# Last product of an encoder layer: quadrant sums of the first visits written into the output tiles, residual added in the second visits

## The chip, the core and the metric

The kernel runs on one core of a Trainium2 chip. The metric is device time in microseconds (us) of one execution; lower is better. Line numbers (L1215 is line 1215) are those of the kernel before the change.

## What is computed

One layer of an encoder over two sequences of 512 tokens with 1024 features: a state-space branch, a differential attention and a cross attention, merged by gates, then a feed-forward part. The change touches the last product of the feed-forward part alone:

```python
x = x + merged @ p['w_out'][l]                       # the residual: x1 in the kernel
xn2 = _rmsnorm(x, p['norm_ffn'][l])
gate, up = jnp.split(xn2 @ p['w_ffn_in'][l], 2, axis=-1)
return x + (jax.nn.silu(gate) * up) @ p['w_ffn_out'][l]   # d_ff = 2816; then a final rmsnorm
```

All arithmetic is in float32. A product is made of three matmuls on split operands (high part times high, high times low, low times high).

## The kernel before

**Data.** Activations lie transposed: 128 features on the partitions, and 1024 columns (two sequences of 512) in a tile. The sum x + merged @ w_out is made tile by tile and kept in device memory as `x1D[0..7]`. The hidden activations of the feed-forward part lie in device memory as `aD[0..21]`.

**The last product** multiplies 22 tiles of hidden activations by `w_ffn_out` into eight output tiles `y[0..7]` (128x1024 each, in four double tiles of the tag `yo`). Eighteen of the 22 hidden tiles go in nine pairs through a scheme of Strassen-Winograd kind: with a pair p of hidden tiles and a pair (m, m+4) of output tiles, seven 512-column products give the four quadrants, a quadrant being one output tile in one sequence. A step with one (m, p) is a **piece**: seven products of three matmuls, so 21 matmuls of 128x128 by 128x512. The last four hidden tiles are multiplied afterwards in the ordinary way (L1240 to L1305), together with the final norm.

**Visits.** `VISITS` (L35) lists twelve visits (m, first pair, end of pairs); below they are called v0 to v11. v0 to v3 are the first visits of m = 0..3 (pairs from 0 on, 2 to 4 pieces), v4 to v7 the second ones (3 pieces each), v8 to v11 the third ones. There are 36 pieces. In a visit seven PSUM banks (six of the tag `mm`, one of `tr`) collect the seven products over the pieces of the visit. Then they are drained (`quadrants`, L1068): ScalarE copies the first bank to `p1`, and seven VectorE additions (`summed`, L1062 to L1066, one PSUM operand and one SBUF operand each) leave the four quadrant sums c11, c22, c21 and c12 in scratch tiles: one of `gf`, one of `up`, two of `nsq`, each tag with two buffers. GpSimd then adds each of the four into its half of `y[m]` or `y[m+4]` (L1213 to L1215, four additions of 128x512 a visit). TensorE starts the next visit while the drain goes on; it needs a bank only when its own turn comes.

**Residual.** In each first visit at pair 1 (L1200 to L1203) two DMAs of 512 KB put `x1D[m]` and `x1D[m+4]` into `y[m]` and `y[m+4]`, so that all quadrant sums are added onto the residual.

**Pairs.** `act_pair` (L1081) loads two hidden tiles (`fa`, `fb`) into the tag `ld`, a ring of four 128x1024 tiles, and makes four sums of quadrants in the tile `ts` (`quad_sums`, L931 to L939: three VectorE operations at L935, L937 and L938, one GpSimd operation at L936). `quad_split` (L947) splits all seven operands into high (ScalarE, L132) and low parts (VectorE, L133). Nine pairs pass in this way; seven of them during the visits. In the text, pair 3's `fb` is the second tile of the fourth pair. After v8 the ring holds the last four hidden tiles (`fl`, L1231).

**Weights.** Pieces 0 to 15 load seven ready-made weight matrices from `wD` (two DMAs, L1165 and L1167). Pieces 16 to 27 load four of the seven, and the raw weights for the other three (L418, L422), which are split on the core (L135 on ScalarE, L136 on VectorE). Pieces 28 to 35 load raw weights alone, whose sums GpSimd makes (L427 to L430). Six tiles (`w_room`, L1150) hold the weights of three pieces, so the load for piece n can go out when piece n-3 is done.

**Order.** All DMAs of this stage are issued by the queue of SyncE (SP), strictly one after the other: a DMA that waits for its tile holds back all that stand behind it. The order in each engine's queue is worked out at build time by a scheduler with a simulated timeline, so an instruction may stand well ahead of its place in the text; `tc.issue_after(i)` keeps an instruction behind i on i's engine, and `queued()` (L283) keeps a DMA behind the last weight load. TensorE's order in the visits is fixed by the text (`PE.on`).

## Time and profile before

| | us |
|---|---|
| median of three runs (lowest, highest) | 1623.96 (1622.52, 1624.75) |
| the profiled execution's own time | 1623.77 |
| its span, first to last instruction | 1622.0 |
| TensorE busy | 1588.7 (98%) |
| VectorE busy | 1170.7 (72%) |
| GpSimd busy | 548.8 (34%) |

The granted TensorE clock of the profiled execution was 0.995 of full speed. Times in the trace count from the start of the span; about 1.8 us of the execution's own time lie outside it. The visits lie between about 1385 and 1564 us. Busy time counts how long instructions ran; TensorE's matmuls are pipelined, so a matmul of 0.39 us may start 0.23 us after the one before. "<-" in a row names what an operation reads, or, behind an idle time, what ended it.

### The profile page before, as it was taken

Reading aid. Unit: us, or ns where it says so; the run is one execution under the profiler, and the core shown is the slowest. Engines: PE = TensorE matmul, PEld = TensorE weight load, DVE = VectorE, ACT = ScalarE, POOL = GpSimd, SP = SyncE. Lnnn points to the kernel's source line nnn. Section 1 sums busy time; section 2 is a strip of 40 time slices with the busy share of each in tenths; the row PEclk is TensorE's granted clock in tenths of the full one; section 3 lists DMA queues with packets and bytes.
Section 4 is the critical chain, followed back from the end, with each engine's and each line's share of the span. In section 5 each row is a group of like instructions: output and inputs, shape, how many; then the busy total and the mean of one; then the engine's idle time right before and its main releaser. Section 6 shows DMA issues by size and latency. Waiting matters only on the chain.

```text
span 1622.0 us, 21561 instructions
## 1 busy us (share of the span) xinstructions
PE 1588.7 (98%) x7812; PEld 1312.7 (81%) x7812; DVE 1170.7 (72%) x1852; ACT 639.0 (39%) x1141; POOL 548.8 (34%) x452
## 2 busy tenths in 40 slices
PE   7999999999999999999999999999999999999997
PEld 6788788888898778777878888888888887777877
DVE  8957897067774666767364668888898877988664
ACT  6534323265553355564123444333233233233233
POOL 0001100000223221300343367666655554444563
PEclk9999999999999999999999999999999999999998
DMA  9354533666763110144454532333333223885322
GB/s 378 119 170 157 147 130 120 180 221 229 247 210 129 53 59 27 50 146 168 139 187 136 154 101 97 126 121 117 119 115 117 83 87 114 324 338 184 98 66 104
DMA packets 104747, 237.84 MB, mean 147 GB/s; under 512 B 13505, under 2 KB 44993, under 8 KB 104641
## 3 DMA queue, kind: packets, MB, share of 16 engines
q1 hardware_dynamic: 104640, 236.47, 42.7%
q8 instruction: 61, 1.00, 0.3%
q14 instruction: 46, 0.37, 0.1%
HBM read 165.16 MB, written 71.27 MB: 146 GB/s over the span
## 4 chain that ended last, share of the span: by engine, by line
PE 74%; DVE 12%; DMA 5%; issue 4%; POOL 2%; ACT 2%; SPq 0%; DVEq 0%; POOLq 0%; ACTq 0%
PE bkmm L64 64%; PE bksc L64 2%; PE bkoo L64 2%; PE bktr L67 2%; DVE wl L133 1%; DVE st L1580 1%; PE bktr L64 1%; DMA yt<-bD 1%; PE bktr L1562 1%; DMA w<-wD 1%; POOL mg L760 1%; DVE tl L133 1%; POOL y L1215 1%; DMA fa<-aD 0%; DMA wf<-in_w_mv 0%
## 5 line engine op out<-in xcount | busy, mean ns | idle before, releaser
L64 PE MATMUL bkmm<-xh,wh 128*128 128x512 f32 x640 | 255.6, 399 | 1.2 <-ACT wh L132 1.2
L64 PE MATMUL bkmm<-xh,wl 128*128 128x512 f32 x640 | 250.8, 392 | 0.0
L64 PE MATMUL bkmm<-xl,wh 128*128 128x512 f32 x640 | 250.7, 392 | 0.0
L64 PE MATMUL bkmm<-th,wl 128*128 128x512 f32 (+1 forms) x621 | 241.3, 389 | 3.0 <-DVE wl L133 3.0
L64 PE MATMUL bkmm<-tl,wh 128*128 128x512 f32 (+1 forms) x621 | 241.8, 389 | 0.6 <-DVE tl L133 0.6
L64 PE MATMUL bkmm<-th,wh 128*128 128x512 f32 (+1 forms) x621 | 241.6, 389 | 0.7 <-ACT th L132 0.7
L132 ACT CAST wh<-wf 128x1024 fp32r<-128x1024 f32 (+1 forms) x133 | 117.7, 885 | 200.5 <-PE bkmm L64 174.0
L133 DVE TENSOR_TENSOR wl<-wf,wh 128x1024 fp32r<-128x1024 f32 (+1 forms) x133 | 147.7, 1111 | 63.6 <-ACT wh L132 54.7
L64 PEld LDWEIGHTS bkmm<-xh,wh 128*128 128x128 f32 x640 | 120.3, 188 | 31.9 <-issue 7.9
L64 PE MATMUL bkmm<-th,w 128*128 128x512 f32 x432 | 141.7, 392 | 4.2 <-DMA w<-wD 2.2
L64 PEld LDWEIGHTS bkmm<-xh,wl 128*128 128x128 f32 x640 | 120.2, 188 | 27.0 <-issue 1.3
L64 PEld LDWEIGHTS bkmm<-th,wl 128*128 128x128 f32 x621 | 116.8, 188 | 27.6 <-DVE wl L133 3.5
L64 PEld LDWEIGHTS bkmm<-xl,wh 128*128 128x128 f32 x640 | 120.5, 188 | 22.3 <-issue 0.4
L64 PEld LDWEIGHTS bkmm<-tl,wh 128*128 128x128 f32 x621 | 116.8, 188 | 25.2 <-DVE tl L133 1.3
L64 PEld LDWEIGHTS bkmm<-th,wh 128*128 128x128 f32 x621 | 116.8, 188 | 24.6 <-ACT th L132 0.8
L427 POOL TENSOR_TENSOR raw<-raw 128x128 f32<-128x128 f32 x28 | 14.9, 531 | 294.7 <-DVE hl L136 262.9
L1127 POOL TENSOR_TENSOR up<-up,acc 128x512 f32<-128x512 f32 x44 | 84.2, 1932 | 77.3 <-DVE up L1065 77.3
L64 PEld LDWEIGHTS bkmm<-th,w 128*128 128x128 f32 x432 | 81.0, 188 | 25.5 <-DVE up L1065 3.3
L1126 ACT ACTIVATE ac<-gf 128x512 f32<-128x512 f32 x44 | 27.8, 633 | 163.8 <-DVE gf L1125 82.7
L760 POOL TENSOR_TENSOR mg<-mg,gl 128x1024 f32<-128x1024 f32 x16 | 43.9, 2743 | 140.0 <-DVE gl L756 140.0
L521 ACT ACTIVATE e<-bksc,nb 128x512 f32<-128x512 f32 (+1 forms) x96 | 58.7, 615 | 71.9 <-DVE nb L516 51.7
L64 PE MATMUL bkmm<-tl,w 128*128 128x512 f32 x216 | 84.2, 390 | 0.0
(638 smaller groups left out, 3606.4 us busy)
## 6 DMA issues: line engine op xcount, KB each, us to landing
wf<-in_w_in SPq DMA_DIRECT2D x40, 512.0 KB, 3.8
wD<-hl SPq DMA_DIRECT2D x28, 512.0 KB, 2.9
w<-wD SPq DMA_DIRECT2D x28, 512.0 KB, 4.7
gD<-gt SPq DMA_DIRECT2D x24, 512.0 KB, 2.9
gl<-gD SPq DMA_DIRECT2D x24, 512.0 KB, 3.4
wf<-in_w_fg SPq DMA_DIRECT2D x22, 512.0 KB, 3.5
wf<-in_w_fu SPq DMA_DIRECT2D x22, 512.0 KB, 3.5
aD<-ac SPq DMA_DIRECT2D x22, 512.0 KB, 2.8
```

The costliest lines, as they stand in the source:

```text
L64: return self.put(self.eng.matmul(*args, **kw))
L67: return self.put(self.eng.transpose(*args, **kw))
L132: h = S.copy(hi, src)
L133: l_ = V.tensor_tensor(out=lo, in0=src, in1=hi.bitcast(F32), op=ALU.subtract)
L427: PO.tensor_tensor(out=a22, in0=a21, in1=a22, op=ALU.add)
L521: last_x = S.activation(out=e, in_=sc, func=AF.Exp, bias=nb, scale=scale, accum_out=sm)
L760: PO.tensor_tensor(out=mg[m], in0=mg[m], in1=gt, op=ALU.add)
L1126: last_t = S.activation(out=ac[:, cs], in_=gf, func=AF.Tanh, scale=0.5)
L1127: PO.tensor_tensor(out=up, in0=up, in1=accs[s], op=ALU.mult)
L1215: PO.tensor_tensor(out=yv, in0=yv, in1=c_, op=ALU.add)
L1562: PE.matmul(ps[:, g * P : (g + 1) * P], w_[:, gg * P : (gg + 1) * P], u_[:, 8 * o + gg, :], start=True, stop=True)
L1580: V.tensor_tensor(out=sv[:, :, :, i], in0=p_, in1=q_, op=ALU.add)
```

## The change

In v0 to v3 the four sums that `quadrants` makes are written by VectorE into the halves of `y[m]` and `y[m+4]` themselves; GpSimd adds nothing there, and `x1D` is not loaded. In v4 to v7, from the visit's first piece on, `x1D[m]` and `x1D[m+4]` are loaded into two tiles of the ring `ld`; after the four quadrant additions of these visits GpSimd adds the two tiles onto `y[m]` and `y[m+4]`, each in one addition of 128x1024. v8 to v11 are as before. The other callers of `quadrants` get the same tiles in the same order.

```diff
     def summed(tag, p_, other, bufs=1):
         nonlocal last_sum
-        t_ = (rp if tag == "nsq" else ap2).tile([P, L], F32, tag=tag, name=tag, bufs=bufs)
+        t_ = tag
+        if isinstance(tag, str):
+            t_ = (rp if tag == "nsq" else ap2).tile([P, L], F32, tag=tag, name=tag, bufs=bufs)
         last_sum = V.tensor_tensor(out=t_, in0=p_, in1=other, op=ALU.add)
         return t_
 
-    def quadrants(ps, p0, other=("up", "gf")):
+    def quadrants(ps, p0, names=("gf", "gf", "up", "up")):
...
-        c11 = summed("gf", next(ps), p1, 2)
+        c11 = summed(names[0], next(ps), p1, 2)
...
-        c22 = summed("up", p5, u3, 2)
-        c21 = summed(other[0], next(ps), u3, 2)
-        return c11, summed(other[1], next(ps), u4, 2), c21, c22
+        c22 = summed(names[3], p5, u3, 2)
+        c21 = summed(names[2], next(ps), u3, 2)
+        return c11, summed(names[1], next(ps), u4, 2), c21, c22
...
-            if v < 4 and p == 1:
+            if 4 <= v < 8 and p == lo_:
+
+                xs = [slot("ld", name="xr") for _ in range(2)]
                 with queued():
-                    for t in (m, m + 4):
-                        nc.sync.dma_start(y[t], x1D[t])
+                    for t, x_ in zip((m, m + 4), xs):
+                        nc.sync.dma_start(x_, x1D[t])
...
-        c11, c12, c21, c22 = quadrants(ps, next(ps), ("nsq", "nsq"))
-        for c_, t, s in ((c11, 0, 0), (c22, 4, 1), (c21, 4, 0), (c12, 0, 1)):
-            yv = y[m + t][:, s * L : (s + 1) * L]
-            PO.tensor_tensor(out=yv, in0=yv, in1=c_, op=ALU.add)
+        yv = [y[m + t][:, s * L : (s + 1) * L] for t in (0, 4) for s in range(NS)]
+        if v < 4:
+            quadrants(ps, next(ps), yv)
+        else:
+            c11, c12, c21, c22 = quadrants(ps, next(ps), ("gf", "nsq", "nsq", "up"))
+            for c_, y_ in ((c11, yv[0]), (c22, yv[3]), (c21, yv[2]), (c12, yv[1])):
+                PO.tensor_tensor(out=y_, in0=y_, in1=c_, op=ALU.add)
+            if v < 8:
+                for t, x_ in zip((m, m + 4), xs):
+                    PO.tensor_tensor(out=y[t], in0=y[t], in1=x_, op=ALU.add)
```

## Prediction

> **What bounds the kernel now.** I read the page first, then the busy times of the last product in thirds, then TensorE's instructions in order of time, looking for every start that comes later than the pace.

> ```profile
> span 1622.0 us, 21561 instructions
> PE 1588.7 (98%) x7812; PEld 1312.7 (81%) x7812; DVE 1170.7 (72%) x1852; ACT 639.0 (39%) x1141; POOL 548.8 (34%) x452
> ```

> TensorE (PE) is busy for 98% of the span. The change lies in the visits, from about 1385 to 1564 us. The next view has, for three stretches of them, the busy time of PE, PEld, VectorE (DVE), ScalarE (ACT) and GpSimd (POOL), the granted clock, the share of the DMA engines and GB/s.

> ```profile
> 1385.00:1444.00 59.00, 56.68 (x247) 45.74 (x246) 53.83 (x59) 17.70 (x22) 28.59 (x18) 1.00 0.95 368
> 1444.00:1503.00 59.00, 58.20 (x255) 47.21 (x254) 50.28 (x63) 18.02 (x26) 27.23 (x20) 1.00 0.64 219
> 1503.00:1565.00 62.00, 60.92 (x265) 49.09 (x264) 41.26 (x54) 17.36 (x28) 38.30 (x50) 1.00 0.23 69
> ```

> PE leaves 2.3, 0.8 and 1.1 us open: 4.2 us in 180. So GpSimd's work, which the change moves about, can give no more than PE's own gaps give. In v0 to v3 (first row) two other things are full: the DMA engines (0.95) and VectorE (53.8 of 59). In v4 to v7 the DMA engines have room (0.64). Now the gaps, in TensorE's rows:

> ```profile
> 1390.75 0.39 PE L64 MATMUL bkmm<-th,w 128*128 128x512 f32 x1
> 1392.25 0.50 PE L64 MATMUL bkmm<-th,w 128*128 128x512 f32 x1 [1.11 <-DMA w<-wD]
> ...
> 1425.49 0.39 PE L64 MATMUL bkmm<-tl,w 128*128 128x512 f32 x1
> 1425.72 0.39 PE L64 MATMUL bkmm<-th,w 128*128 128x512 f32 x1
> 1427.23 0.47 PE L64 MATMUL bkmm<-th,w 128*128 128x512 f32 x1 [1.12 <-DMA w<-wD]
> ...
> 1462.71 0.39 PE L64 MATMUL bkmm<-th,w 128*128 128x512 f32 x1
> 1463.85 0.50 PE L64 MATMUL bkmm<-th,w 128*128 128x512 f32 x1 [0.76 <-DVE up L1065]
> ...
> 1506.99 0.39 PE L64 MATMUL bkmm<-th,w 128*128 128x512 f32 x1
> 1507.71 0.50 PE L64 MATMUL bkmm<-th,w 128*128 128x512 f32 x1 [0.32 <-DVE up L1065]
> ```

> The pace is 1425.72 - 1425.49 = 0.23 us from start to start, so a piece of 21 matmuls takes 4.8 us and a visit of three 14.3. Against it the four places lose 1.27 (v0), 1.28 (first piece of v3), 0.91 (first piece of v5) and 0.49 us (first piece of v8): 3.95 us. The first two wait for weights, the other two for VectorE, which has not yet emptied a PSUM bank of the visit before.

> **What is removed: 16 GpSimd additions and eight DMAs in v0 to v3.**

> ```profile
> L1215 POOL TENSOR_TENSOR y<-y,nsq 128x512 f32<-128x512 f32 x22 | 34.8, 1594 | 2.4 <-DVE nsq L1065 2.4
> L1215 POOL TENSOR_TENSOR y<-y,up 128x512 f32<-128x512 f32 x12 | 16.9, 1408 | 10.9 <-DVE up L1065 10.9
> ...
> y<-x1D SPq DMA_DIRECT2D x8, 512.0 KB, 7.0
> ```

> At about 1.5 us each, 16 additions are 24 us of GpSimd. It isn't on TensorE's path there, so by itself that is worth nothing. What counts is whom they hold up. VectorE's rows with a GpSimd addition beside them and without one, and the additions themselves:

> ```profile
> 1399.44 2.31 DVE L133 TENSOR_TENSOR tl<-fb,th 128x1024 fp32r<-128x1024 f32 x1
> 1414.29 2.31 DVE L133 TENSOR_TENSOR tl<-fb,th 128x1024 fp32r<-128x1024 f32 x1
> 1416.52 1.77 DVE L937 TENSOR_TENSOR ts<-fb,ts 128x512 f32<-128x512 f32 x1
> 1418.33 0.69 DVE L938 TENSOR_TENSOR ts<-fb,ts 128x512 f32<-128x512 f32 x1
> 1439.89 1.21 DVE L133 TENSOR_TENSOR tl<-fb,th 128x1024 fp32r<-128x1024 f32 x1
> ...
> 1402.86 2.26 POOL L1215 TENSOR_TENSOR y<-y,nsq 128x512 f32<-128x512 f32 x1
> 1430.44 1.29 POOL L1215 TENSOR_TENSOR y<-y,up 128x512 f32<-128x512 f32 x1
> ```

> The same split takes 1.21 us alone and 2.31 us beside an addition; the addition takes 1.29 alone and 2.26 beside a split. Each loses about what the other needs. Now SP's queue ahead of the second gap:

> ```profile
> 1414.44 0.32 SPq L1084 DMA_DIRECT2D fa<-aD  x1
> 1419.12 0.32 SPq L1085 DMA_DIRECT2D fb<-aD  x1
> 1419.54 0.37 SPq L1167 DMA_DIRECT2D w<-wD  x1
> 1419.96 0.42 SPq L1203 DMA_DIRECT2D y<-x1D  x1
> 1420.48 0.38 SPq L1165 DMA_DIRECT2D w<-wD  x1
> ...
> SPq L1085 <- DVE ts L938: 5.2, 2, 4.3
> ```

> SP stood for 4.3 us at pair 5's `fb`, until L938 of pair 3 had freed its tile. Two weight loads stood behind it, and the second also behind a residual load (512 KB at 368 GB/s: 1.4 us). Those weights came at 1427.1. Without the additions L133 (1414.29) and L937 (1416.52) are 1.1 us shorter each, and so is one L133 of pair 2 ahead of them. I take 3 us less of standing, and 1.4 us less of transfer in front. Gap two needs 1.28. **Gap two goes: -1.3 us** (bounds -1.4 and 0).

> Gap one stays: the first residual load is issued at 1391.42, when the late weights (issued at 1384.78) are almost there. 0 us (bounds -1.3, if the new queue order helps them, and 0).

> VectorE's writes into `y` instead of the scratch tiles have the same size and operands, so 0 us, hidden under TensorE in any case. No one waits for them before v4's additions.

> **What is added: eight loads and eight GpSimd additions of 128x1024 in v4 to v7.** The nearest row of that shape:

> ```profile
> L760 POOL TENSOR_TENSOR mg<-mg,gl 128x1024 f32<-128x1024 f32 x16 | 43.9, 2743 | 140.0 <-DVE gl L756 140.0
> ```

> That is 2 x 2.74 = 5.5 us a visit (bounds 5.2, four times 1.29, and 9.1, four times 2.26). GpSimd has 27.2 us of work in the 59 us of v4 to v7, and gets to 49: it isn't the bound. The loads add 4.2 MB to 59 us at 219 GB/s, which makes 290, under the 368 seen in v0 to v3; 0 us. If they came in front of a late weight load, each would cost it 1.4 us.

> Three things are queued behind the new waits.

> (a) *VectorE beside the longer additions.* Its splits of weights and pairs can each lose up to 2.7 us instead of 1.3. VectorE has 59 - 50.3 = 8.7 us open there, and only the bank drains touch TensorE; an L1065 reads one operand from PSUM and keeps its 0.68 us. I take +0.3 us (bounds 0 and +3).

> [...]

> (b) *The ring `ld`.* The loads take two of its four tiles in each of v4 to v7, so pair 7 has to wait for v5's residual additions and pair 8 for pair 7. In the trace these pairs have long been loaded.

> ```profile
> 1465.12 3.19 POOL L1215 TENSOR_TENSOR y<-y,nsq 128x512 f32<-128x512 f32 x2
> ```

> v4's four additions end at 1468.3. Two residual additions end at 1474 and v5's at 1488. Pair 7 is then loaded by 1494, taking 5 to 6 us, and split by about 1501; pair 8 by 1507 and 1514. Pair 8 is first needed in the fourth piece of v8, which starts after 1507.7 + 2 x 4.8 = 1517 or a little later. Three us are left, so 0 us (bounds 0 and +4).

> (c) *The sums of the pairs in the drains.* The gap of 0.91 us stands where the sums of a pair were put between the drain's additions:

> ```profile
> 1457.10 1.78 DVE L935 TENSOR_TENSOR ts<-fa 128x512 f32<-128x512 f32 x1
> 1458.81 0.68 DVE L1065 TENSOR_TENSOR u<-bkmm,p 128x512 f32<-128x512 f32 x1
> 1461.20 1.39 DVE L938 TENSOR_TENSOR ts<-fb,ts 128x512 f32<-128x512 f32 x1
> 1463.12 0.67 DVE L1065 TENSOR_TENSOR up<-bkmm,u 128x512 f32<-128x512 f32 x1
> ```

> These are pair 7's; they now come two visits later. Gap three goes (-0.9). Gap four, at the start of v8, comes with the work for `fl`, which now also moves back (-0.5). The same sums now lie in the drains of v6 and v7; I take between the two gaps, 0.45 us, for each, +0.9. Net **-0.5 us** (bounds -1.4 and +0.9).

> **Sum.** -1.3 + 0.3 - 0.5 = **-1.5 us**: 1622.3 against the profiled execution's 1623.77, whose span of 1622.0 has 1.8 us around it. The median of the runs is 0.2 us higher, so I give **1622.5 us**; the likeliest case alone reaches from 1621.0 to 1623.3. A measurement of this kernel can tell about 0.2%, 3.2 us, from no change, so this counts as the same.

> **Rivals.**

> *SP stands at a residual load (slower).* In v5 and v7 the new loads wait for GpSimd's residual additions of the visit before. v5 starts at 1460.2 (11 matmuls of 0.23 us before the row of 1462.71); the second of v4's tiles is free at 1474, 13.6 us later. If the queue has the loads where the text has them, behind the third weight load of the visit, all later weights stand there. A weight load may go out two pieces, 9.5 us, ahead of its use, and takes 5.1 us to land:

> ```profile
> w<-wD SPq DMA_DIRECT2D x26, 512.0 KB, 5.1
> ```

> So 4.4 us of standing are free, and the rest, up to 9 us in each of v5 and v7, is TensorE's. It decides from 4.4 us of standing on. Against it: the queue has pair loads where their tiles come free, not where the text has them, and the longest standing at one was 4.3 us. For it: that one cost gap two. With half of the standing in one visit it is 1622.5 + 4.5 = 1627, with all of it in one 1631.5. Chance 0.18.

> *VectorE blocked by the long additions (slightly slower).* Two more blocks of 2.7 us in a visit put 5.4 us on VectorE in each of v4 to v7, 21.6 in all against 8.7 us open. It would be 13 us short if each addition hit a split; a quarter of that, with drains late, is +3: 1625.5. It decides from 8.7 us of blocking on. Chance 0.12. [...]

> *All four gaps go (faster).* The queues are worked out anew, the first weights come ahead of pair 3's loads, and no pair's sums fall into a drain: -3.95, so 1620.0, and with the smaller losses at other drains 1619.3. Chance 0.22.

> *No effect.* Gap two comes from SP's standing alone and stays, or comes back elsewhere: 1623.3 to 1624.5. Chance 0.12.

> **How the numbers follow.** The forecast keeps 0.36. Faster by over 0.2% (under 1620.7) are the third rival and 0.02 of the forecast: 0.24. Slower by over 0.2% (over 1627.2) are most of the first rival, 0.17, and 0.03 of the second: 0.20. The same: 0.56. The range of 1619.3 to 1628.5 leaves out about half of the first rival and a third of the third, near 0.2.

> **What would show it.** In the changed kernel's trace: no TensorE idle put down to DMA w<-wD in v3; DMA share clearly under 0.95 in v0 to v3 and over 0.64 in v4 to v7; L133 near 1.2 us in v0 to v3; residual additions of 2.6 to 3 us; SP's longest standing at a residual load under 4.4 us; pair 8 split before v8's fourth piece. The forecast is wrong if TensorE waits for weights in v5 to v8, for pair 8 in v8, or longer than 1 us for a drain in v4 to v7.

## The result and the profile after

The changed kernel takes 1639.31 us (median; 1637.38 to 1642.51), the kernel before beside it 1622.39 us (1621.32 to 1624.75; six runs of each, three of the six before are those of the table above). The ratio is 1.0103, interval 1.0092 to 1.0114: 17 us slower, outside the range of 1619.3 to 1628.5. The profiled execution took 1637.38 us.

The page of the changed kernel:

```profile
span 1635.6 us, 21557 instructions
PE 1593.0 (97%) x7812; PEld 1313.6 (80%) x7812; DVE 1172.0 (72%) x1852; ACT 639.1 (39%) x1141; POOL 552.9 (34%) x444
```

The busy times hardly moved; the span grew by 13.6 us. Up to the visits both kernels issue the same instructions in the same order, and yet this execution is 5 us ahead of the one before when the visits begin (1380.0 against 1385.2). The other kernels of this document share that part too, and in their traces the visits begin at 1381 to 1385 us, so I take the 5 us as scatter. Traces are therefore compared below by the **length of the visits**, from TensorE's first matmul of the first piece to its first matmul behind the last piece: 178.8 us before, 197.5 us after, +18.7.

Where they lie is seen by cutting both traces at the start of v4. The view gives the busy times of a stretch (length; PE, PEld, DVE, ACT, POOL; clock, DMA share, GB/s). v4 to v11 of the kernel before:

```profile
1445.60:1564.00 118.40, 116.52 (x507) 94.13 (x506) 89.10 (x112) 34.87 (x53) 63.62 (x67) 1.00 0.42 140
```

and of the changed kernel:

```profile
1439.30:1577.40 138.10, 124.49 (x506) 97.28 (x505) 97.63 (x111) 34.27 (x53) 85.91 (x72) 0.95 0.48 161
```

v4 to v11 became 19.7 us longer, v0 to v3 1.1 us shorter (60.4 to 59.3). Of the 19.7 us, 11.7 are time in which PE stands (138.10 - 124.49 = 13.6, against 1.9), and 8.0 are more busy time of the same matmuls. The clock of 0.95 in place of 1.00 accounts, by my estimate, for at most 6.9 of these 8.0 (0.05 of 138.1). GpSimd has 22.3 us more work, VectorE 8.5.

v0 to v3 and v4 to v7 of the changed kernel, for the DMA shares:

```profile
1380.00:1439.00 59.00, 57.71 (x252) 46.62 (x251) 50.19 (x64) 17.70 (x22) 9.56 (x6) 1.00 0.79 281
1439.00:1505.00 66.00, 59.33 (x244) 47.46 (x243) 44.50 (x50) 14.43 (x22) 37.84 (x20) 0.95 0.64 222
```

The DMA share fell from 0.95 to 0.79 in v0 to v3, as forecast. In v4 to v7 it stayed at 0.64, where more was forecast. DMA bandwidth is not what ran out. The waits, from 1380 to 1580 us (total, times, longest), of the changed kernel:

```profile
ACT th L132 <- DMA fa<-aD: 19.1, 4, 12.0
DVE ts L935 <- DMA fa<-aD: 11.2, 3, 7.0
ACT th L135 <- DMA fl<-aD: 9.0, 2, 7.2
PE bkmm L64 <- DVE u L1067: 4.4, 3, 2.2
PE bkmm L64 <- ACT p L1073: 4.0, 1, 4.0
...
PE bkmm L64 <- DVE up L1067: 3.1, 2, 2.9
PE bkmm L64 <- DMA w<-wD: 1.1, 1, 1.1
```

and of the kernel before (1380 to 1565 us):

```profile
ACT th L132 <- DMA fa<-aD: 2.6, 1, 2.6
PE bkmm L64 <- DMA w<-wD: 2.2, 2, 1.1
PE bkmm L64 <- DVE up L1065: 1.2, 3, 0.8
```

One of the two weight waits is gone: gap two. In its place ScalarE and VectorE wait for pairs (`fa`) and for the last tiles (`fl`), and TensorE waits for the drain (L1067 and L1073 are L1065 and L1071 of before; lines behind them have moved as well, so L1086 is L1084 of before).

**How a late pair stops TensorE.** SP's queue at the start of v4, and its later pair loads:

```profile
1440.06 0.42 SPq L1207 DMA_DIRECT2D xr<-x1D  x1
1440.59 0.59 SPq L1086 DMA_DIRECT2D fa<-aD  x1
...
1482.10 0.38 SPq L1086 DMA_DIRECT2D fa<-aD  x1
...
1503.92 0.37 SPq L1086 DMA_DIRECT2D fa<-aD  x1
```

Pairs 6, 7 and 8 are asked for 60.6, 102.1 and 124.0 us after the visits began. Before (L1084: 1433.63, 1439.43, 1453.37) it was 48.5, 54.3 and 68.2. Pair 6 is not needed until the third piece of v7, so it is not late for TensorE. But its first operations stand in the queues of ScalarE

```profile
1448.66 0.62 ACT L132 CAST th<-fa 128x512 fp32r<-128x512 f32 x1 [12.02 <-DMA fa<-aD]
...
1450.82 1.05 ACT L132 CAST th<-ts 128x1024 fp32r<-128x1024 f32 x1
1451.76 0.58 ACT L1073 COPY p<-bkmm 128x512 f32<-128x512 f32 x1
```

and VectorE, ahead of the drain of v4 and between its additions:

```profile
1448.60 0.69 DVE L935 TENSOR_TENSOR ts<-fa 128x512 f32<-128x512 f32 x1 [7.00 <-DMA fa<-aD]
...
1453.85 1.21 DVE L133 TENSOR_TENSOR tl<-ts,th 128x1024 fp32r<-128x1024 f32 x1
1454.98 0.68 DVE L1067 TENSOR_TENSOR u<-bkmm,p 128x512 f32<-128x512 f32 x1
1455.59 0.67 DVE L1067 TENSOR_TENSOR gf<-bkmm,p 128x512 f32<-128x512 f32 x1
1456.18 1.21 DVE L133 TENSOR_TENSOR tl<-ts,th 128x1024 fp32r<-128x1024 f32 x1
1457.32 1.61 DVE L136 SCALAR_TENSOR_TENSOR w<-acc,w 128x384 fp32r<-128x384 f32 x1
1458.85 0.68 DVE L1067 TENSOR_TENSOR u<-bkmm,u 128x512 f32<-128x512 f32 x1
```

ScalarE stands 12.0 us, VectorE 7.0. Then both work off the pair, in the order of their queues, and the drain has to wait in line: its first addition comes 2.6 us after the copy of the first bank (1451.76 + 0.58), the third 2.6 us after the second ended. TensorE, in v5's first piece:

```profile
1455.72 0.50 PE L64 MATMUL bkmm<-th,w 128*128 128x512 f32 x1 [1.37 <-DVE u L1067]
...
1459.58 0.50 PE L64 MATMUL bkmm<-th,w 128*128 128x512 f32 x1 [2.20 <-DVE u L1067]
```

The largest single stop, in v9's first piece, has the same form on ScalarE. One tile of `fl` was late, and the copy of v8's first bank stood behind it:

```profile
1530.53 1.06 ACT L135 ACTIVATE th<-fl 128x1024 fp32r<-128x1024 f32 x1 [7.22 <-DMA fl<-aD]
...
1533.37 0.56 ACT L1073 COPY p<-bkmm 128x512 f32<-128x512 f32 x1
```

TensorE waited 3.95 us for that copy. This much can be read; whether it is the ring alone, or also the longer GpSimd additions, can't.

### The profile page after: what moved, and what is told of

It is laid out like the page before. It is cut to its first block, busy times and chain, and to the rows that moved or that the text cites. A ratio compares the mean times of both kernels' runs of the same rounds, so it can differ in the third digit from the quotient of the medians.

```text
span 1635.6 us, 21557 instructions
## 1 busy us (share of the span) xinstructions
PE 1593.0 (97%) x7812; PEld 1313.6 (80%) x7812; DVE 1172.0 (72%) x1852; ACT 639.1 (39%) x1141; POOL 552.9 (34%) x444
## 4 chain that ended last, share of the span: by engine, by line
PE 77%; DVE 12%; DMA 4%; issue 3%; POOL 2%; ACT 1%; SPq 0%; DVEq 0%; POOLq 0%; ACTq 0%
PE bkmm L64 67%; PE bksc L64 2%; PE bkoo L64 2%; PE bktr L67 2%; DMA fa<-aD 1%; DVE wl L133 1%; DVE tl L133 1%; DVE st L1590 1%; PE bktr L1572 1%; PE bktr L64 1%; POOL y L1222 1%; DMA w<-wD 1%; DVE w L136 1%; DMA wf<-in_w_mv 0%; DVE xt L250 0%
## 5 line engine op out<-in xcount | busy, mean ns | idle before, releaser
L64 PE MATMUL bkmm<-xh,wh 128*128 128x512 f32 x640 | 255.5, 399 | 1.2 <-ACT wh L132 1.2
L64 PE MATMUL bkmm<-xh,wl 128*128 128x512 f32 x640 | 250.7, 392 | 0.0
L64 PE MATMUL bkmm<-xl,wh 128*128 128x512 f32 x640 | 250.6, 392 | 0.0
L64 PE MATMUL bkmm<-th,wl 128*128 128x512 f32 (+1 forms) x621 | 241.0, 389 | 2.8 <-DVE wl L133 2.8
L64 PE MATMUL bkmm<-th,wh 128*128 128x512 f32 (+1 forms) x621 | 241.1, 389 | 0.7 <-ACT th L132 0.7
L64 PE MATMUL bkmm<-tl,wh 128*128 128x512 f32 (+1 forms) x621 | 241.2, 388 | 0.6 <-DVE tl L133 0.6
L133 DVE TENSOR_TENSOR wl<-wf,wh 128x1024 fp32r<-128x1024 f32 (+1 forms) x133 | 147.8, 1111 | 63.3 <-ACT wh L132 54.6
L64 PE MATMUL bkmm<-th,w 128*128 128x512 f32 x432 | 146.7, 403 | 14.8 <-DVE u L1067 4.4
L64 PEld LDWEIGHTS bkmm<-xh,wh 128*128 128x128 f32 x640 | 120.3, 188 | 31.8 <-issue 7.9
L64 PEld LDWEIGHTS bkmm<-xh,wl 128*128 128x128 f32 x640 | 120.2, 188 | 27.0 <-issue 1.3
L64 PEld LDWEIGHTS bkmm<-xl,wh 128*128 128x128 f32 x640 | 120.4, 188 | 22.3 <-issue 0.4
L64 PEld LDWEIGHTS bkmm<-th,wl 128*128 128x128 f32 x621 | 116.5, 188 | 27.0 <-DVE wl L133 3.2
L64 PEld LDWEIGHTS bkmm<-tl,wh 128*128 128x128 f32 x621 | 116.6, 188 | 25.1 <-DVE tl L133 1.3
L64 PEld LDWEIGHTS bkmm<-th,wh 128*128 128x128 f32 x621 | 116.6, 188 | 24.8 <-ACT th L132 0.8
L64 PEld LDWEIGHTS bkmm<-th,w 128*128 128x128 f32 x432 | 82.9, 193 | 40.1 <-DVE u L1067 6.4
L427 POOL TENSOR_TENSOR raw<-raw 128x128 f32<-128x128 f32 x28 | 14.9, 532 | 291.1 <-DVE hl L136 260.1
L760 POOL TENSOR_TENSOR mg<-mg,gl 128x1024 f32<-128x1024 f32 x16 | 43.9, 2746 | 138.9 <-DVE gl L756 138.9
L64 PE MATMUL bkmm<-tl,w 128*128 128x512 f32 x216 | 86.0, 398 | 0.1
## 6 DMA issues: line engine op xcount, KB each, us to landing
wf<-in_w_in SPq DMA_DIRECT2D x40, 512.0 KB, 3.8
wD<-hl SPq DMA_DIRECT2D x28, 512.0 KB, 2.9
w<-wD SPq DMA_DIRECT2D x28, 512.0 KB, 4.5
gD<-gt SPq DMA_DIRECT2D x24, 512.0 KB, 2.9
gl<-gD SPq DMA_DIRECT2D x24, 512.0 KB, 3.4
wf<-in_w_fg SPq DMA_DIRECT2D x22, 512.0 KB, 3.5
wf<-in_w_fu SPq DMA_DIRECT2D x22, 512.0 KB, 3.4
aD<-ac SPq DMA_DIRECT2D x22, 512.0 KB, 2.8
```

The source lines that it names most:

```text
L64: return self.put(self.eng.matmul(*args, **kw))
L133: l_ = V.tensor_tensor(out=lo, in0=src, in1=hi.bitcast(F32), op=ALU.subtract)
L760: PO.tensor_tensor(out=mg[m], in0=mg[m], in1=gt, op=ALU.add)
```

## The experiments

Theory R: the loss comes from the two residual loads in the ring `ld`, since they make pairs late. Theory A: it comes from the eight long additions on GpSimd, which slow VectorE (step a). Each ratio is against the kernel before beside it. "Visits" is their length in the one trace of each kernel. The wait for weights in v0 alone is 1.1 to 2.7 us in these traces, so differences of visits under 2 us are not read.

| kernel | ring holds x1D | long additions on | ratio [95%] | visits, us |
|---|---|---|---|---|
| before | no | none | 1 | 178.8 |
| after | yes | GpSimd | 1.0103 [1.0092, 1.0114] | 197.5 |
| e3_no_residual | no | none | 0.9990 [0.9978, 1.0001] | 175.3 |
| e7_own_tile_short_adds | no | none | 0.9976 [0.9965, 0.9986] | 176.6 |
| e2_short_adds | yes | none | 1.0088 [1.0072, 1.0104] | 195.2 |
| e4_before_ring | yes | none | 1.0103 [1.0083, 1.0122] | 195.8 |
| e1_own_tile | no | GpSimd | 1.0065 [1.0050, 1.0080] | 187.8 |
| e5_own_tile_in_visit | no | GpSimd | 1.0048 [1.0032, 1.0065] | 186.3 |
| e8_before_adds | no | GpSimd | 1.0054 [1.0039, 1.0069] | 190.6 |
| e13_own_tile_halves | no | GpSimd | 1.0057 [1.0042, 1.0071] | 185.3 |
| e6_ring_in_visit | yes | GpSimd | 1.0064 [1.0048, 1.0081] | 192.3 |
| e12_own_tile_dve | no | VectorE | 1.0004 [0.9991, 1.0018] | 181.4 |
| e14_own_tile_dve_after | no | VectorE | 1.0017 [1.0007, 1.0027] | 182.7 |
| e15_short_adds_order | yes | none | 1.0005 [0.9994, 1.0016] | 181.3 |
| e9_order | yes | GpSimd | 1.0101 [1.0079, 1.0123] | 197.6 |
| e10_own_tile_order | no | GpSimd | 1.0084 [1.0069, 1.0100] | 191.9 |
| e11_before_order | no | none | 1.0011 [0.9999, 1.0023] | 180.9 |

### One part of the change at a time

e1 keeps the change but loads x1D into the scratch tile `ac`, one tile at a time, and leaves the ring alone. e2 keeps the ring and adds 8 columns only. e3 leaves the residual of this product out. e4 is the kernel before with the change's ring loads, each read in 8 columns.

```diff
# e1
-                xs = [slot("ld", name="xr") for _ in range(2)]
+                xs = ap2.tile([P, NT], F32, tag="ac", name="xr")
...
+                PO.tensor_tensor(out=y[m], in0=y[m], in1=xs, op=ALU.add)
+                xs = ap2.tile([P, NT], F32, tag="ac", name="xr")
+                with queued():
+                    nc.sync.dma_start(xs, x1D[m + 4])
+                PO.tensor_tensor(out=y[m + 4], in0=y[m + 4], in1=xs, op=ALU.add)
# e2
-                    PO.tensor_tensor(out=y[t], in0=y[t], in1=x_, op=ALU.add)
+                    PO.tensor_tensor(out=y[t][:, :8], in0=y[t][:, :8], in1=x_[:, :8], op=ALU.add)
# e3
-            if 4 <= v < 8 and p == lo_:
+            if False:
...
-            if v < 8:
+            if False:
# e4, against the kernel before
+            if 4 <= v < 8 and p == lo_:
+                xs = [slot("ld", name="xr") for _ in range(2)]
+                with queued():
+                    for t, x_ in zip((m, m + 4), xs):
+                        nc.sync.dma_start(x_, x1D[t])
...
+        if 4 <= v < 8:
+            for t, x_ in zip((m, m + 4), xs):
+                PO.tensor_tensor(out=y[t][:, :8], in0=y[t][:, :8], in1=x_[:, :8], op=ALU.add)
```

> The change, but the residual tiles pass through a tile of their own (the scratch tile ac, idle in the visits), one after the other, and not through the ring ld. Theory (ring): the loss of 17 us comes from the ring, because pairs and the last hidden tiles are loaded late and ScalarE and VectorE stand at them with the drain behind; then this kernel takes 1619 to 1623 us. Rival (GpSimd): the additions of 128x1024 block VectorE and make the drains late; they are all still here, so 1634 to 1640 us.

> The change, but each residual addition takes 8 of the 1024 columns (the rest of the residual is left out of the output); loads and ring as in the change. Theory (ring): the tiles are held until after the drain as before, only some 5 us less in a visit, so most of the loss stays: 1631 to 1638 us. Rival (GpSimd): the long additions are gone, so 1619 to 1623 us.

> The change without loading or adding the residual at all (it is left out of the output): only the writing of the first visits' sums into the output tiles is left. Both theories: no late pairs and no long additions, and the wait for weights in v3 gone, so 1618.5 to 1621 us; over 1624 would mean that the writes themselves cost something.

> The kernel before, with two more loads of x1D into the ring ld in each of v4 to v7, read by GpSimd in 8 columns after the four quadrant additions (which adds the residual a second time in 8 columns of each output tile). Theory (ring): the loads alone bring the loss, 1632 to 1640 us. Rival (GpSimd): nothing is long on GpSimd, so 1622 to 1625 us. A third view, that the loss needs the whole new order, gives something between, 1625 to 1630 us.

e3 shows that the loss lies in the residual's new place: without it the kernel is level with the one before, and its visits are 3.5 us shorter. e2 and e4 show that the **ring alone** is enough for nearly all of it, without a long addition and even in the kernel before. e4's VectorE, in the drain of v4:

```profile
1461.27 0.67 DVE L1065 TENSOR_TENSOR gf<-bkmm,p 128x512 f32<-128x512 f32 x1
1461.87 1.21 DVE L133 TENSOR_TENSOR tl<-ts,th 128x1024 fp32r<-128x1024 f32 x1
1463.00 1.61 DVE L136 SCALAR_TENSOR_TENSOR w<-acc,w 128x384 fp32r<-128x384 f32 x1
1464.53 0.68 DVE L1065 TENSOR_TENSOR u<-bkmm,u 128x512 f32<-128x512 f32 x1
```

It is the order of the changed kernel, and TensorE stops 2.21 us for that last `u`. But e1, without the ring, still loses 0.65%. So R alone isn't the whole either.

### The long additions by themselves

e5 and e6 put the additions right behind the loads, inside the visit, and none behind the drain: e5 with its own tile, in the first two pieces, e6 with the change's two ring tiles, both in the first piece. e7 is e1 with additions of 8 columns. e8 is the kernel before with two additions of 128x1024 into the scratch tile `ac` in each of v4 to v7; nothing reads them.

```diff
# e5
+            if 4 <= v < 8 and p < lo_ + 2:
+                t = m + 4 * (p - lo_)
+                xs = ap2.tile([P, NT], F32, tag="ac", name="xr")
                 with queued():
+                    nc.sync.dma_start(xs, x1D[t])
+                PO.tensor_tensor(out=y[t], in0=y[t], in1=xs, op=ALU.add)
# e6, against the change, behind the two loads
+                for t, x_ in zip((m, m + 4), xs):
+                    PO.tensor_tensor(out=y[t], in0=y[t], in1=x_, op=ALU.add)
# e7, against e1
-                PO.tensor_tensor(out=y[m], in0=y[m], in1=xs, op=ALU.add)
+                PO.tensor_tensor(out=y[m][:, :8], in0=y[m][:, :8], in1=xs[:, :8], op=ALU.add)
# e8, against the kernel before
+        if 4 <= v < 8:
+            for t in (m, m + 4):
+                PO.tensor_tensor(out=ac, in0=ac, in1=y[t], op=ALU.add)
```

> The change with the tile of its own, and each residual addition right behind its load, in the first two pieces of the visit, ahead of the drain. The additions then meet fewer of VectorE's bank drains and don't stand in front of the quadrant additions: if the drains are what the long additions hurt, 1621 to 1627 us; if any long addition beside a pair's split costs the same, 1628 to 1634 us.

> The change with the ring, but the two residual additions right behind their loads at the visit's first piece, not behind the drain: the two tiles are held some 8 us in a visit in place of 15 to 20. Theory (ring, held too long): pairs come in time more often, 1623 to 1632 us. If holding two of four tiles at all is what counts: 1634 to 1641 us.

> The residual through the tile of its own, as in the run with the own tile (1632.7 us), but each residual addition takes 8 of 1024 columns (the rest of the residual is left out). What was left of the loss there is laid to the long GpSimd additions, which block VectorE's splits and sums and the raw weight sums behind them on GpSimd. If so: 1619 to 1622 us. If the eight loads themselves cost (the queue of SP standing at the second load, 3 to 5.5 us in the trace of that run): 1627 to 1633 us.

> The kernel before, with two more GpSimd additions of 128x1024 after the four quadrant additions in each of v4 to v7, from y into a scratch tile whose content nothing reads again; no load, no ring. If the long additions alone cost, as in the run with the own tile: 1628 to 1633 us. If they cost only together with late data: 1621 to 1624 us.

e8 shows that the **additions alone** cost 0.54%, 9 us, in a kernel with nothing else changed, and e7 against e1 puts them at about 0.9% (1.0065 / 0.9976) in the changed one. e7 against e2 (0.9976, 1.0088) is the ring by itself, at the same short additions. e6 is quicker than the changed kernel (1.0064): its tiles come back to the ring sooner, which speaks for R. But the additions moved as well, and in e6's trace the clock stays at 1.00 in v4 to v11, so it is no clean test. The stretch of v4 to v11 in e8:

```profile
1444.30:1573.40 129.10, 119.00 (x505) 93.21 (x504) 102.12 (x112) 34.42 (x53) 86.06 (x75) 1.00 0.39 128
```

Against the row of the kernel before, GpSimd has 22.4 us more work, and VectorE, which was given none, 13.0 more. PE stands 10.1 us in place of 1.9. How that reaches TensorE is seen in e1. VectorE in the drain of v6:

```profile
1487.77 0.68 DVE L1067 TENSOR_TENSOR u<-bkmm,p 128x512 f32<-128x512 f32 x1
1488.37 2.24 DVE L937 TENSOR_TENSOR ts<-fb,ts 128x512 f32<-128x512 f32 x1
1490.53 0.68 DVE L1067 TENSOR_TENSOR gf<-bkmm,p 128x512 f32<-128x512 f32 x1
```

and GpSimd:

```profile
1487.26 2.80 POOL L1226 TENSOR_TENSOR y<-y,xr 128x1024 f32<-128x1024 f32 x1
...
1525.56 2.39 POOL L1226 TENSOR_TENSOR y<-y,xr 128x1024 f32<-128x1024 f32 x1 [1.12 <-DMA xr<-x1D]
1527.91 0.46 POOL L429 TENSOR_TENSOR acc<-acc 128x128 f32<-128x128 f32 x1
```

The drain's own additions keep 0.68 us. The sum of a pair that stands between two of them (L937, 0.68 us alone) takes 2.24 beside the residual addition and ends 0.55 us after it, and TensorE stops 1.80 us for `gf`. The second GpSimd row shows another way: the raw weight sums (L427 to L430) stand behind a residual addition that waits for its load. ScalarE's operation on those weights waits for them, the copy of the drain waits behind it, and TensorE stops 1.68 us for the copy.

### Another engine, other sizes

e12 is e5 with the additions on VectorE, e14 is e1 with them on VectorE, e13 is e1 with each addition cut into two of 512 columns.

```diff
# e12, against e5 (e14, against e1, in both places)
-                PO.tensor_tensor(out=y[t], in0=y[t], in1=xs, op=ALU.add)
+                V.tensor_tensor(out=y[t], in0=y[t], in1=xs, op=ALU.add)
# e13, against e1, in both places
-                PO.tensor_tensor(out=y[m], in0=y[m], in1=xs, op=ALU.add)
+                for h in (slice(0, L), slice(L, NT)):
+                    PO.tensor_tensor(out=y[m][:, h], in0=y[m][:, h], in1=xs[:, h], op=ALU.add)
```

> [...] If GpSimd's blocking was the cost: 1619 to 1624 us. If VectorE has no room, so that drains come late: 1626 to 1633 us.

> The own tile (1632.7 us), each long addition cut into two of 512 columns: the same GpSimd work in pieces of 1.3 us. If the length of a single blocking addition is what hurts VectorE: 1623 to 1628 us. If the total of GpSimd work beside VectorE's is: 1630 to 1634 us.

> The own tile, additions on VectorE behind the drain of their visit in place of the first pieces (1623.9 us there). Placed behind the drains they delay no bank: 1618 to 1621 us, faster than before. If they push splits of weights or pairs back: 1623 to 1628 us.

On VectorE, with its own tile, the residual costs nothing that can be told from the kernel before (e12) or 0.17% (e14). The group of e12's additions (count, busy us, mean ns, idle before):

```profile
L1207 DVE TENSOR_TENSOR y<-y,xr 128x1024 f32<-128x1024 f32 x8 | 10.8, 1355 | 11.2 <-DMA xr<-x1D 11.2
```

and of the changed kernel's:

```profile
L1225 POOL TENSOR_TENSOR y<-y,xr 128x1024 f32<-128x1024 f32 x8 | 21.5, 2707 | 0.2
```

10.8 us of VectorE's own time cost less here than 21.5 us of GpSimd's beside it (e12's 1.0004 against e5's 1.0048); in e8 such additions came with 13.0 us more on VectorE. Halves make no difference that can be told (e13's 1.0057 against e1's 1.0065), so the length of a single addition is not what costs here.

### The order in the queues

If R acts through the order, it must vanish when the work of late pairs is kept behind the drain. e9 does that in the changed kernel for pairs 5 to 8 and the splits of `fl`, e10 in e1, e11 in the kernel before (what the order itself costs), e15 in e2.

```diff
-        S.copy(p1, p0)
+        nonlocal last_p
+        last_p = S.copy(p1, p0)
...
-            pair_in()
+            with tc.issue_after(last_sum.ins), tc.issue_after(last_p.ins):
+                pair_in()
...
-                split(th, tl, ac, scale=0.5)
+                with tc.issue_after(last_sum.ins), tc.issue_after(last_p.ins):
+                    split(th, tl, ac, scale=0.5)
```

> The change with its ring and its long additions, but the sums and splits of pairs 5 to 8, and the splits of the last four hidden tiles, kept behind the drain of the visit before them on VectorE and ScalarE. Theory: the loss comes about because drains stand in the two queues behind work on tiles that land late; with the drains in front TensorE gets its banks and 1620 to 1628 us are left, the rest by pairs that come too late for their own piece. If lateness or blocking counts by itself whatever the order: 1634 to 1641 us.

> The own tile (1632.7 us with the long additions) and the same order. If the long additions hurt only through sums and splits that stand between the additions of a drain: 1617 to 1622 us, faster than before. If they hurt through the splits of weights and the raw weight sums behind them on GpSimd: 1626 to 1633 us.

> The kernel before with the same order: its drains of v4 and v7 lose 0.9 and 0.5 us to work that stands in between. If that is all there is to gain: 0.5 to 1.5 us under the kernel before; if pairs come late for their piece: 0 to 3 us over it.

> The change with its ring, additions of 8 columns only (the rest of the residual is left out; 1636.6 us without the order) and the pairs' work kept behind the drain. With the long additions gone the ring is alone. If its loss comes because drains stand behind work on late tiles: 1620 to 1626 us. If the lateness itself reaches TensorE by pairs and weights that come too late: 1630 to 1638 us.

For the ring alone it holds: e15 is at 1.0005, where e2 was at 1.0088. The order itself gains nothing: in the kernel before it gives 1.0011 (e11), level with it. e15's pair loads are still late (pairs 6 to 8 are asked for 62.9, 91.9 and 108.9 us after the visits began), and its visits take 181.3 us. TensorE's waits in it:

```profile
PE bkmm L64 <- DVE w L136: 4.2, 1, 4.2
PE bkmm L64 <- DMA w<-wD: 2.7, 1, 2.7
```

No wait for a drain is left; one for a weight split that now stands behind the work for `fl` is new. For the whole change it fell: I had expected the order to mend e9 too, and it is where the changed kernel was (1.0101), while e10 is slower than e1. The pair work that was put behind the drain now meets GpSimd's additions there. In e9 the sums of pair 7 stand behind the drain of v6, and so do the residual additions of v6. GpSimd, VectorE, ScalarE and TensorE, up to v8's first piece:

```profile
1499.35 6.18 POOL L1226 TENSOR_TENSOR y<-y,xr 128x1024 f32<-128x1024 f32 x2
1500.40 2.87 DVE L937 TENSOR_TENSOR ts<-fb,ts 128x512 f32<-128x512 f32 x1
1503.30 1.06 ACT L132 CAST th<-ts 128x1024 fp32r<-128x1024 f32 x1 [7.59 <-DVE ts L937]
...
1508.01 0.56 ACT L1074 COPY p<-bkmm 128x512 f32<-128x512 f32 x1
1508.62 0.50 PE L64 MATMUL bkmm<-th,w 128*128 128x512 f32 x1 [3.29 <-ACT p L1074]
```

Beside the residual additions the sum (L937) takes 2.87 us; in e15, which has no long additions, the same sum takes 0.68. ScalarE stands 7.59 us for it, the copy of v7's first bank stands behind, and TensorE stops 3.29 us for that copy. e9's longest stop, 5.42 us in v9, is for a weight split behind the splits of `fl`. e15 has this one too (the 4.2 us above; three splits of `fl` take 6.07 us in e9 and 6.09 in e15), so it comes with the order and not with the long additions.

## Why the prediction was wrong

- **Gap two goes, -1.3 us: right.** No weight wait is left in v3, and v0 to v3 are 1.1 us shorter. Gap one stayed (1.1 us), as forecast. The writes into `y` take 0.68 us, so 0 was right. e3 (visits -3.5 us; its ratio of 0.9990 can't be told from 1) and e7 (-0.24%) show what was to be had of it, up to 4 us, but both leave out the residual's additions.
- **Step (b), the ring at 0 us (bounds 0 and +4), is the step that failed.** It asked only whether a pair is split before TensorE *uses* it, and there it held, if barely: TensorE never waited for pair 8, although it was split at 1527.2 and not at 1514, 3.4 us after v8's fourth piece had begun (1523.8). It did not ask what stands *behind* the pair's first operation on ScalarE and VectorE. That was the drain of another visit. In place of 0 us, the ring alone costs 0.88 to 1.03%, 14 to 17 us (e2, e4), and with the drains kept in front 0.05% (e15 against e2). Shown.
- **Step (c), -0.5 us, had the mechanism and the wrong size.** It named sums of pairs in drains as the cause of gap three, and let them move to v6 and v7 at 0.45 us each. Sums and splits of pairs came into the drains of v4, v6 and v7, after a load that was late as well, with stops of 1.37 and 2.20 us (v5), 2.87 (v7) and 0.79 (v8).
- **Step (a), the long additions at +0.3 us (bounds 0 and +3), was mis-sized some thirty times:** 0.54% or 9 us (e8). The argument was that the drain's additions, which read PSUM, keep their 0.68 us. They did (means of 0.68 in e8). But it is not so that only the drains touch TensorE: sums, and splits of pairs and weights, stand between the drain's additions in the same queue, and those are what grew: in e1 a sum (L937) took 2.24 us beside a residual addition, against 0.68 alone. Why it grows, and the drain's additions do not, is not shown.
- **The rivals.** That SP stands at a residual load did not happen: SP's longest standing there was 2.4 us, under the 4.4 from which it decides. That VectorE loses time to the long additions did happen: 13.0 us more of busy time in e8. But its condition, more blocking than open time, is not what made the loss: in v4 to v7 themselves VectorE was busy 53.9 of 62.1 us, so 8.2 were still open. Its price of +3 us was a third of what e8 cost. No rival had the late pairs in the queues.
- **The list of what would show it** worked in its last part: it said that the forecast is wrong if TensorE waits longer than 1 us for a drain in v4 to v7. Two of its signs were missed, the DMA share over 0.64 and pair 8 split before v8's fourth piece.

Both causes are shown to suffice alone, at 0.9 to 1.0% for the ring and 0.5 to 0.9% for the long additions. They don't add up (1.03% together; why is not shown). Why the order mends one but not both is told from one trace (e9), not tried further. No kernel with the whole residual beats the one before: the best, e12, is level with it.

## What to carry to other kernels

When tiles of a shared ring are given to someone else, list for every later load of that ring the first instruction that waits for it on each engine, and what stands behind that instruction in the queue: a load can be in time for its use and still stop a drain (here pair 6's, with stops of 1.37 and 2.20 us). Price GpSimd's work beside a busy VectorE as time of VectorE too (here 22.4 us more on GpSimd came with 13.0 more on VectorE, e8), and try VectorE itself where its own time for the same work is shorter (here 10.8 us against 21.5). An average of open time says little (8.2 us were open in v4 to v7 of e8, which lost 9); the instructions between two additions of a drain say more.

## What the runs showed of the hardware

That TensorE's stops cost more than their idle time was not expected. After the stops of 1.37 and 2.20 us the changed kernel's matmuls run at half the clock for a while (busy times and, third from the end, the granted clock):

```profile
1457.78:1461.19 3.41, 1.38 (x5) 0.86 (x6) 3.41 (x5) 0.00 (x0) 1.12 (x2) 1.00 0.57 195
1461.20:1464.61 3.41, 3.41 (x10) 2.63 (x9) 1.37 (x3) 0.52 (x1) 3.41 (x4) 0.50 0.07 19
```

and the starts in the second of these stretches:

```profile
1462.31 0.63 PE L64 MATMUL bkmm<-tl,w 128*128 128x512 f32 x1
1462.74 0.63 PE L64 MATMUL bkmm<-th,w 128*128 128x512 f32 x1
```

They are 0.43 us apart in place of 0.23. The length of a stop alone does not decide this. e6 has stops of 1.41 and 2.19 us in the same place, and keeps its clock:

```profile
1462.90:1466.31 3.41, 1.67 (x6) 1.05 (x6) 3.41 (x4) 0.00 (x0) 2.11 (x1) 1.00 0.94 356
1466.32:1469.72 3.40, 2.27 (x9) 1.58 (x10) 3.23 (x6) 0.00 (x0) 1.22 (x1) 1.00 0.36 115
```

In e1 the matmuls slowed (starts 0.43 us apart from 1531.7 us on) behind a stop of 1.68 us, while in e8, with stops of up to 1.9 us, the clock of v4 to v11 was 1.00.

Near one half the idle share does not tell the cases apart: in e6's first stretch it is 0.51, and the clock stayed, but in the 3.41 us ahead of e1's slow matmuls it is 0.49. What decides there is not shown. The idle time is that between matmul records, whose ends are modelled.
